# Products of a pair in program order, merges' stores on SyncE, convolution inputs five jobs apart: one change to a decoder trunk in Strassen-like pairs

## The chip, the cores and the metric

The kernel runs on one core of a Trainium2 chip. The metric is the time of one execution in device microseconds (us); lower is better. The program is compiled once, and the inputs are those of the reference.

## The reference, cut to what matters

One layer over a sequence of 1024 rows and a width of 1024, in f32: a layer norm with a shift and a scale from `c`, one wide input projection, three branches, a gated merge, an output projection and a last layer norm.

```python
u = layer_norm(x) * (1 + scale) + shift
proj = u @ w_in + b_in
a_v, a_g, b_b, b_c, b_h, b_g, c_a, c_b, c_g, merge = jnp.split(proj, SPLIT_IDX, axis=-1)
pooled = causal_multiscale_pool(a_v)                       # windows 2, 4, 8, 16
y_a = jnp.einsum("bsgi,gio->bsgo", pooled, pool_w).reshape(bsz, slen, W_BRANCH)
y_a = y_a * pool_scale * jax.nn.silu(a_g)
y_b = b_b * causal_dwconv(b_c * b_h, sc_w, sc_b) * jax.nn.silu(b_g)      # 3 taps
h_c = causal_dwconv(c_a * jax.nn.sigmoid(c_b), cf_w, cf_b)               # 31 taps
y_c = jax.nn.silu(layer_norm(h_c, cf_ln_g, cf_ln_b)) * jax.nn.silu(c_g)
m = sum(sigmoid(merge)[k] * (y_k @ w_branch[k]))                         # k = a, b, c
x_new = layer_norm(ALPHA * x + gate * (m @ w_out))
```

## The kernel before, in words

Channels lie on the 128 partitions, the sequence on the free axis. An f32 product is made of three TensorE matmuls: each operand is split into a high and a low part, and `mm3` (L129) multiplies low by high, high by low and high by high, 128x128 weights against 128x512 columns.

The work is a list of **jobs**. Four classic jobs come first (their order is written out by hand). Then come 46 **pairs**: each makes two blocks of 128 channels of the projection at once, with seven products where eight would be needed, from sums of weight blocks and sums of blocks of `u`. A product is 12 matmuls of 128x512 (four blocks of the contraction by three), so a pair is 84. The pairs are `b0`..`b7` and `d0`..`d7` (branch B), `c2`..`c7` (the inputs of the 31-tap convolution; the first two blocks are the classic jobs), `cg` (its gates), `a0`..`a7` (branch A) and `m` (merge gates). After the pairs come the merges: `z1_0`..`z1_7` with the four `pool` jobs between the first of them, then `z0_0`..`z0_7`, then `z2_0`..`z2_7` (the digit behind z is the branch: 0 is A, 1 is B, 2 is C; a z job is 48 matmuls, a pool job 24). Last come the output projection and the last norm.

A pair (class `Pair`, L434 to L542) has two parts. **Its weights** are made in `step` while an earlier pair multiplies: the raw columns come on the SyncE (SP) queue; VectorE (DVE) makes four sums of half tiles; for each of the weight tiles `wa`, `wb`, `wc` and `wd` ScalarE (ACT) writes the high part (L506) and VectorE the low part (L508). `wa`, `wb` and `wc` share one pool of three buffers. **Its products** (`run`, L520 to L542) go into three PSUM banks, `px`, `pz` and `py`. Between products the partial result is taken over: into the tiles `r1` and `r2` by ACT with the bias (L525, L530 and L534) or by DVE additions (L528, L536, L538). Six banks serve the pairs, so those of the pair after next take over those of this one; within a pair `px` is reused, first after A11 B11 (ACT, L525), then after S3 T3 (DVE, L536), and A22 T4 must wait for that addition.

The 31-tap convolutions are DVE work that has no place of its own: `conv_step` (L601) is called once after each job and issues `TAPS` = 6 taps (L610, each an operation on 128x1024) of the convolution at the head of a list; a convolution takes five jobs. Finished convolutions are summed: the first is copied on ACT into a new tile `hsum` (L620), the others are added by DVE, and each is stored to `h_dram`.

The order of instructions on each engine comes from the framework's scheduler, which sorts by dependencies and its own estimate of when each operand is there; `after(ins, mark)` adds a dependency and so an order. The jobs' order is a list built at L877 to L893: c pairs are put in at every `every`-th place.

The DMA queues concerned: all loads of weights are issued on SP. Loads of intermediate results and most stores are issued on POOL (`store`, L543, whose default is `nc.gpsimd`): pooled values and the gates `sga` back from DRAM (`a_load`, L654, with `load_split`, L732), `y` tiles for the merges (also L734), and the stores of `h_dram`, `pool_dram`, `g_dram`, `y_dram` and `c_dram`. A queue issues in order; a store that waits for its data holds what stands behind it. After the loads ACT makes the high part of each `y` or `pool` tile (L129), DVE the low part (L130). `c_rstd` (L800 and L210 to L214) makes the 1/std of branch C's norm, its last step on POOL.

Of the kernel before, what the change touches and what calls it, by code (L numbers as in the profile page):

```python
# [11 lines left out]
AF = mybir.ActivationFunctionType  # L12
# [7 lines left out]
NT = D // P  # L20
# [39 lines left out]
def kernel(  # L60
# [16 lines left out]
    nc = tc.nc  # L77
# [15 lines left out]
    LEFT, RIGHT = slice(0, HALF), slice(HALF, S)  # L93
    HALVES = (LEFT, RIGHT)

    def slot(name, dt=F32):
        return big.tile([P, D], dt, tag="big", name=name)
# [14 lines left out]
    marks = {}  # L112
# [19 lines left out]
    def mm3(ps, wh, wl, rh, rl, start, stop):  # L132
        for n, (w, r) in enumerate(((wl, rh), (wh, rl), (wh, rh))):
            nc.tensor.matmul(  # L134
                ps, w, r, start=start and n == 0, stop=stop and n == 2, skip_group_check=True
            )


    ident = const.tile([P, P], F32, name="ident")
# [308 lines left out]
    def bias(col):  # L448
        return bin_cols[:, col // P : col // P + 1]

    class Pair:
# [26 lines left out]
        def step(self, what):  # L478

            raw1, raw2 = self.raw  # L480
            a1, a2 = (r.rearrange("p (i q c) -> p q i c", q=2, c=P) for r in self.raw)
            if what[0] == "S":
                t = wsum.tile([P, 2, HALF], F32, tag="sum", name=f"s{what[1:]}_{self.name}")
                self.sums[what[1]] = t.rearrange("p n c -> p (n c)")
                one, two = (t[:, n].rearrange("p (i c) -> p i c", c=P) for n in range(2))
                if what == "S12":
                    nc.vector.tensor_add(one, a2[:, 0], a2[:, 1])
                    nc.vector.tensor_sub(two, one, a1[:, 0])
                    self.s2 = two
                else:  # L490
                    nc.vector.tensor_sub(one, a1[:, 0], a2[:, 0])
                    nc.vector.tensor_sub(two, a1[:, 1], self.s2)
                return
            which, high = what[1], what[2] == "h"
            if high and which == "d":
                self.w[which] = wlast.tile([P, 2, HALF], F32R, tag="last", name=f"wd_{self.name}")
            elif high:
                self.w[which] = wspl.tile([P, 2, D], F32R, tag="w", name=f"w{which}_{self.name}")
            hi, lo = (self.w[which][:, n] for n in range(2))
            if which == "d":  # L500
                src = a2[:, 1]
                hi, lo = (t.rearrange("p (i c) -> p i c", c=P) for t in (hi, lo))
            else:
                src = raw1 if which == "a" else self.sums["1" if which == "b" else "3"]
            if high:
                nc.scalar.activation(hi, src, AF.Identity)  # L506
            else:
                marks["split"] = nc.vector.tensor_tensor(  # L508
                    out=lo, in0=src, in1=f32(hi), op=ALU.subtract
                )  # L510

        def product(self, ps, left, right, first):
            which, block = self.left[left]
            w = self.w[which]
            for i in range(4):
                ks = slice(block(i) * P, (block(i) + 1) * P)
                rh, rl = quarter(right, i)
                mm3(ps, w[:, 0, ks], w[:, 1, ks], rh, rl, first and i == 0, i == 3)

        def run(self):  # L520
            col1, col2 = self.cols
            px, pz = bank(f"px_{self.name}"), bank(f"pz_{self.name}")
            r1, r2 = slot(f"r1_{self.name}"), slot(f"r2_{self.name}")
            self.product(px, "A11", "B11", True)
            nc.scalar.activation(r1[:, LEFT], px, AF.Identity, bias=bias(col1))  # L525
            py = bank(f"py_{self.name}")
            self.product(py, "A12", "B21", True)
            nc.vector.tensor_add(r1[:, LEFT], py, r1[:, LEFT])  # L528
            self.product(pz, "S1", "T1", True)
            marks["pair"] = nc.scalar.activation(  # L530
                r2[:, RIGHT], pz, AF.Identity, bias=bias(col2)
            )
            self.product(px, "S2", "T2", False)
            nc.scalar.activation(r1[:, RIGHT], px, AF.Identity, bias=bias(col1))  # L534
            self.product(px, "S3", "T3", False)
            nc.vector.tensor_add(r2[:, RIGHT], px, r2[:, RIGHT])  # L536
            self.product(pz, "S4", "B22", False)
            nc.vector.tensor_add(r1[:, RIGHT], pz, r1[:, RIGHT])  # L538
            self.product(px, "A22", "T4", False)
            self.after(r1, px, r2)  # L540

    def store(dst, src, q=None):  # L542
        return (q or nc.gpsimd).dma_start(out=dst, in_=src)  # L543
# [18 lines left out]
    conv = {"n": 0, "sum": None}  # L562
# [36 lines left out]
    def conv_step(n):  # L599
        while n > 0 and conv_todo:  # L600
            item = conv_todo[0]  # L601
            j, g, h, s = item
            w = cfw_cols[:, (K31 - 1 - s) * NT + j : (K31 - 1 - s) * NT + j + 1]
            if s == 0:
                h = item[2] = slot(f"h{j}")
                ins = nc.scalar.activation(h, g, AF.Identity, bias=vec("cf_b", j), scale=w)  # L606
                if j == 0:
                    after(ins, marks["u"])
            else:
                nc.vector.scalar_tensor_tensor(  # L610
                    out=h[:, s:], in0=g[:, : S - s], scalar=w, in1=h[:, s:],
                    op0=ALU.mult, op1=ALU.add,
                )
                n -= 1
            item[3] = s + 1
            if s == K31 - 1:
                conv_todo.popleft()
                if conv["sum"] is None:
                    conv["sum"] = slot("hsum")
                    nc.scalar.copy(conv["sum"], h)  # L620
                else:
                    nc.vector.tensor_add(conv["sum"], conv["sum"], h)
                store(h_dram[j], h)
                conv["n"] += 1
# [35 lines left out]
    def a_pool(g):  # L660
        def run(w):
            for o in range(2):
                ct = 2 * g + o
                ps = [bank(f"pool_ps{ct}_{h}") for h in range(2)]
                for i in range(2):
                    for h in range(2):
                        ph, pl = pooled[2 * g + i]
                        ws = slice((2 * i + o) * P, (2 * i + o + 1) * P)
                        mm3(
                            ps[h], w[:, 0, ws], w[:, 1, ws], ph[:, HALVES[h]], pl[:, HALVES[h]],  # L670
                            i == 0, i == 1,
                        )
                t = sg_a.pop(ct)
                for h in range(2):
                    nc.vector.scalar_tensor_tensor(  # L675
                        out=t[:, HALVES[h]], in0=ps[h], scalar=vec("pool_scale", ct),
                        in1=t[:, HALVES[h]], op0=ALU.mult, op1=ALU.mult,
                    )
                store(y_dram[0][ct], t)

        jobs.append(Job(f"pool{g}", pool_w[0][g], None, None, run=run))

# [81 lines left out]
    c_dram = dram_tiles("c_dram", NT)  # L764
# [5 lines left out]
    def c_square(j):  # L770
        t = c_state.pop(("h", j))
        nc.vector.tensor_sub(t, t, c_state["mean"])
        store(c_dram[j], t)
        sq = slot(f"sq{j}")
        nc.scalar.activation(sq, t, AF.Square)
        if j == 0:
            c_state["q"] = sq
        else:
            nc.vector.tensor_add(c_state["q"], c_state["q"], sq)
# [28 lines left out]
    def c_y(ct):  # L808
        n, sg = c_state.pop(("y", ct))
        nc.vector.tensor_mul(n, n, c_state["rb"])  # L810
        nc.scalar.activation(
            n, n, AF.Silu, bias=vec("cf_ln_b", ct), scale=vec("cf_ln_g", ct)
        )
        nc.vector.tensor_mul(n, n, sg)
        store(y_dram[2][ct], n)


    y, m, m_hi, m_lo, g_in = {}, {}, {}, {}, {}
# [38 lines left out]
    for b in (1, 0, 2):  # L857
        for i in range(NT // 2):
            light.append(
                lambda b=b, i=i: gates(  # L860
                    f"m{b}_{i}", C_M + b * D + 2 * i * P, AF.Sigmoid, g_dram[b][2 * i : 2 * i + 2],
                    nc.sync if (b, i) == (2, NT // 2 - 1) else None,
                )
            )
    heavy = [f for group in todo for f in group]
# [5 lines left out]
            order.append(light[li])  # L871
            li += 1
    order += light[li:]
    every = 6
    j = CLASSIC // 2
    for n, f in enumerate(order):
        if n % every == every - 1 and j < NT:  # L877
# [94 lines left out]
    for i, job in enumerate(jobs):  # L972
# [10 lines left out]
            f(*args)  # L983
        if 8 <= i < 8 + NT:
            gate_row(i - 8)
        if n_proj <= i < n_proj + 8 and (i - n_proj) % 2 == 0:
            a_load((i - n_proj) // 2)
        if i == n_a - 2:
            marks["y0"] = marks["split"]
            for k in range(NT):  # L990
# [91 lines left out]
```

## Time and profile before

| | us |
|---|---|
| median of three runs | 1385.55 (1384.88 to 1387.03) |
| the profiled execution | 1386.24 |
| its span (first to last instruction) | 1384.5 |
| PE busy in the span | 1330.3 (96%) |
| DVE busy | 1099.0 (79%) |
| ACT busy | 527.5 (38%) |
| POOL busy | 113.0 (8%) |

The span is cut in 40 slices in the profile, and PE's busy digits are 9 in nearly all of them; DVE's are 9 from about 35 to 450 us and 4 to 9 behind that. The share of DMA engines is under 5 tenths from about 70 to 970 us and 6 to 9 tenths for the 240 us behind it, where the merges load and store. A matmul's record shows its duration from start to modelled end, and matmuls overlap, so what a matmul costs is read from starts, or from a stretch divided by the number of them.

### The profile page before, as it was taken

The page shows a single profiled execution, that of the slowest core. Times are in us where ns is not written, and L with a number is a line of the kernel's source. Part 1 is how long each engine was busy: PE and PEld are TensorE (multiplying, and loading weights), DVE is VectorE, ACT ScalarE, POOL GpSimd, SP SyncE. Part 2 cuts the span into 40 slices and gives each one's busy share as a digit, 9 for nine tenths or more (in the row PEclk, how much of TensorE's full clock was granted, in tenths as well). Part 3 has the DMA queues.
Part 4 walks back from the last instruction along what each step waited for, and adds up shares of the span by engine and source line. Part 5 has one row for each costly group of instructions (what it writes and reads, how often), then busy time and mean ns, then how long its engine had stood idle before and what let it go on. Part 6 is the DMA issues. An engine that isn't in the chain of part 4 may idle for free. (4 is left out here: it accounts for less than half of the span.)

```text
span 1384.5 us, 15237 instructions
## 1 busy us (share of the span) xinstructions
PE 1330.3 (96%) x5893; PEld 1097.3 (79%) x5893; DVE 1099.0 (79%) x1292; ACT 527.5 (38%) x652; POOL 113.0 (8%) x220
## 2 busy tenths in 40 slices
PE   4999799999999999999999999999897999999997
PEld 3778688887888888888888888888685888888886
DVE  7999999999999589958975998699645657645576
ACT  6554244434443444435343543444422333313100
POOL 2000000000000000000000000000212232200010
PEclk9999999999999999999999999999998999999999
DMA  9511323443222313222342234224868979712332
GB/s 320 158 46 47 106 76 94 131 126 107 65 88 95 104 46 108 98 69 79 111 146 77 76 119 139 92 84 137 311 227 281 341 274 335 273 61 77 122 107 92
DMA packets 167949, 188.40 MB, mean 136 GB/s; under 512 B 6292, under 2 KB 138820, under 8 KB 167876
## 3 DMA queue, kind: packets, MB, share of 16 engines
q1 hardware_dynamic: 141936, 94.91, 23.1%
q0 software_dynamic: 25408, 92.29, 17.9%
q8 instruction: 46, 0.75, 0.2%
q10 hardware_dynamic: 532, 0.22, 0.1%
q14 instruction: 27, 0.22, 0.0%
HBM read 137.06 MB, written 50.34 MB: 135 GB/s over the span
## 5 line engine op out<-in xcount | busy, mean ns | idle before, releaser
L610 DVE SCALAR_TENSOR_TENSOR h<-r_c,cfw_cols,h 128x1023 f32<-128x1023 f32 (+9 forms) x180 | 226.9, 1261 | 5.5 <-ACT h L606 5.3
L610 DVE SCALAR_TENSOR_TENSOR h<-cs,cfw_cols,h 128x1023 f32<-128x1023 f32 (+29 forms) x60 | 75.8, 1263 | 1.3 <-ACT h L606 1.0
L832 DVE TENSOR_TENSOR g<-ps_z,g 128x512 f32<-128x512 f32 x48 | 31.7, 687 | 51.6 <-PE ps_z L134 51.1
L408 ACT ACTIVATE w_z<-raw_z 128x1024 fp32r<-128x1024 f32 x24 | 25.2, 1060 | 124.3 <-PE ps_z L134 62.3
L134 PE MATMUL ps_p<-u,w_p 128*128 128x512 f32 x192 | 48.8, 409 | 0.6 <-DVE u L346 0.6
L134 PEld LDWEIGHTS ps_p<-u,w_p 128*128 128x128 f32 x192 | 36.8, 196 | 8.8 <-DVE u L346 1.7
L414 DVE TENSOR_TENSOR w_z<-raw_z,w_z 128x1024 fp32r<-128x1024 f32 x24 | 29.1, 1220 | 14.6 <-ACT w_z L408 14.6
L543 POOL DMA_DIRECT2D g_dram<-r_m x22 | 11.7, 532 | 349.4 <-ACT r_m L718 238.1
L134 PE MATMUL py_m<-u,wa_m 128*128 128x512 f32 x144 | 36.2, 389 | 0.0
L134 PE MATMUL ps_z<-y_3h,w_z 128*128 128x512 f32 x96 | 34.0, 391 | 1.7 <-ACT y_3h L129 1.7
L134 PE MATMUL ps_z<-y_0h,w_z 128*128 128x512 f32 x96 | 35.4, 403 | 0.0
L134 PE MATMUL px_m<-u,wa_m 128*128 128x512 f32 x144 | 34.8, 389 | 0.0
L134 PE MATMUL pz_m<-u,wc_m 128*128 128x512 f32 x144 | 34.6, 389 | 0.0
L134 PE MATMUL ps_z<-y_1h,w_z 128*128 128x512 f32 x96 | 34.0, 389 | 0.0
L134 PE MATMUL ps_z<-y_2h,w_z 128*128 128x512 f32 x96 | 33.8, 389 | 0.0
L134 PE MATMUL ps_z<-y_4h,w_z 128*128 128x512 f32 x96 | 33.5, 389 | 0.0
L134 PE MATMUL ps_z<-y_7h,w_z 128*128 128x512 f32 x96 | 33.3, 389 | 0.0
L134 PE MATMUL ps_z<-y_6h,w_z 128*128 128x512 f32 x96 | 33.3, 389 | 0.0
L134 PE MATMUL ps_z<-y_5h,w_z 128*128 128x512 f32 x96 | 33.3, 389 | 0.0
L1032 DVE TENSOR_TENSOR og<-out_ps,gate_b 128x512 f32<-128x512 f32 (+1 forms) x18 | 11.1, 624 | 26.7 <-PE out_ps L134 13.4
L134 PE MATMUL px_m<-t_1h,wb_m 128*128 128x512 f32 x96 | 32.1, 389 | 0.0
L134 PE MATMUL pz_m<-t_0h,wb_m 128*128 128x512 f32 x96 | 31.5, 389 | 0.0
(567 smaller groups left out, 3879.7 us busy)
## 6 DMA issues: line engine op xcount, KB each, us to landing
raw_m<-in_w_in_dram SPq DMA_DIRECT2D x24, 512.0 KB, 4.0
raw_z<-in_w_branch_dram SPq DMA_DIRECT2D x24, 512.0 KB, 10.3
g<-g_dram POOLq DMA_DIRECT2D x24, 512.0 KB, 8.2
g_dram<-r_m POOLq DMA_DIRECT2D x22, 512.0 KB, 3.6
ada<-in_w_ada_dram SPq DMA_DIRECT2D x32, 256.0 KB, 6.4
raw_b<-in_w_in_dram SPq DMA_DIRECT2D x16, 512.0 KB, 4.0
raw_d<-in_w_in_dram SPq DMA_DIRECT2D x16, 512.0 KB, 4.0
raw_a<-in_w_in_dram SPq DMA_DIRECT2D x16, 512.0 KB, 4.0
```

Source lines behind the costliest of these rows:

```text
L134: nc.tensor.matmul(ps, w, r, start=start and n == 0, stop=stop and n == 2, skip_group_check=True)
L408: nc.scalar.activation(self.w[:, 0, : self.width], raw, AF.Identity)
L414: marks["split"] = nc.vector.tensor_tensor(out=lo, in0=raw, in1=f32(hi), op=ALU.subtract)
L543: return (q or nc.gpsimd).dma_start(out=dst, in_=src)
L610: nc.vector.scalar_tensor_tensor(out=h[:, s:], in0=g[:, : S - s], scalar=w, in1=h[:, s:], op0=ALU.mult, op1=ALU.add,)
L832: nc.vector.tensor_mul(g[:, HALVES[h]], ps[h], g[:, HALVES[h]])
L1032: nc.vector.tensor_mul(t, ps[q], final["gate"][:, sl])
```

## The change

It has six parts.

1. `chained` takes the place of `mm3` in a pair's products: the first matmul of each product depends on the last of the product before it, so that PE takes the products as the program lists them. In `run` the product S2 T2 and its eviction now stand ahead of S1 T1, which now stands between S2 T2 and S3 T3.
2. ACT's high parts of `wa`, `wb` and `wc` are kept in their program order (not `wd`).
3. The copy of the first finished convolution into `hsum` is gone; the convolution's own tile is the sum.
4. The stores of `y_dram[0]` (from the pool jobs), `c_dram` and `y_dram[2]` are issued on SP, and with them four of the `g_dram` stores of branch C's gates where it was two.
5. `every` is 5 where it was 6: pairs `c2` to `c7` come earlier, the last convolution is done six to seven jobs sooner, and what lies between them shifts.
6. `a_load(0..3)` is called one job earlier each.

```diff
+    def chained(ps, wh, wl, rh, rl, first, start, stop):
+
+        for n, (w, r) in enumerate(((wl, rh), (wh, rl), (wh, rh))):
+            ins = nc.tensor.matmul(
+                ps, w, r, start=start and n == 0, stop=stop and n == 2, skip_group_check=True
+            )
+            if n == 0 and first and "product" in marks:
+                after(ins, marks["product"])
+        if stop:
+            marks["product"] = ins
...
             if high:
-                nc.scalar.activation(hi, src, AF.Identity)
+                ins = nc.scalar.activation(hi, src, AF.Identity)
+                if "high" in marks and which != "d":
+                    after(ins, marks["high"])
+                if which != "d":
+                    marks["high"] = ins
...
-                mm3(ps, w[:, 0, ks], w[:, 1, ks], rh, rl, first and i == 0, i == 3)
+                chained(ps, w[:, 0, ks], w[:, 1, ks], rh, rl, i == 0, first and i == 0, i == 3)
...
+            self.product(px, "S2", "T2", False)
+            nc.scalar.activation(r1[:, RIGHT], px, AF.Identity, bias=bias(col1))
             self.product(pz, "S1", "T1", True)
             marks["pair"] = nc.scalar.activation(
                 r2[:, RIGHT], pz, AF.Identity, bias=bias(col2)
             )
-            self.product(px, "S2", "T2", False)
-            nc.scalar.activation(r1[:, RIGHT], px, AF.Identity, bias=bias(col1))
...
                 if conv["sum"] is None:
-                    conv["sum"] = slot("hsum")
-                    nc.scalar.copy(conv["sum"], h)
+                    conv["sum"] = h
...
-                store(y_dram[0][ct], t)
+                store(y_dram[0][ct], t, nc.sync)
...
-        store(c_dram[j], t)
+        store(c_dram[j], t, nc.sync)
...
-        store(y_dram[2][ct], n)
+        store(y_dram[2][ct], n, nc.sync)
...
-                    nc.sync if (b, i) == (2, NT // 2 - 1) else None,
+                    nc.sync if b == 2 and i >= NT // 2 - 2 else None,
...
-    every = 6
+    every = 5
...
-        if n_proj <= i < n_proj + 8 and (i - n_proj) % 2 == 0:
-            a_load((i - n_proj) // 2)
+        if n_proj - 1 <= i < n_proj + 7 and (i - n_proj) % 2 == 1:
+            a_load((i - n_proj + 1) // 2)
```

How the change moves instructions, at three places. A name's last number counts tiles; lines behind the change are 11 to 15 higher.

**ACT, at the first pair `b0`** (`r_b` are its results, `px_b` and `pz_b` its banks, `wd_b` its last weight tile; `wb_d` and `wa_c` are weights of the pair that follows). Before:

```order
L506 ACTIVATE wd_b_1248<-raw_b_1_1103 128x512
L557 ACTIVATE r_cg_1254<-px_cg_1251,bin_cols 128x512
L506 ACTIVATE wb_d_1370<-s_d_1367 128x1024
L620 COPY hsum<-h_955 128x1024
L525 ACTIVATE r_b_1384<-px_b_1382,bin_cols 128x512
L530 ACTIVATE r_b_1385<-pz_b_1383,bin_cols 128x512
L606 ACTIVATE h_1482<-cs_856,vec_cols,cfw_cols 128x1024
```

and now:

```order
L517 ACTIVATE wd_b_1248<-raw_b_1_1103 128x512
L572 ACTIVATE r_cg_1254<-px_cg_1251,bin_cols 128x512
L540 ACTIVATE r_b_1382<-px_b_1380,bin_cols 128x512
L517 ACTIVATE wa_c_1362<-raw_c_0_1229 128x1024
L545 ACTIVATE r_b_1382<-px_b_1380,bin_cols 128x512
L517 ACTIVATE wb_c_1368<-s_c_1365 128x1024
L547 ACTIVATE r_b_1383<-pz_b_1381,bin_cols 128x512
```

The copy into `hsum` stood between the weights of `d0` and the first eviction of `b0`; now only evictions and the weights of `c2`, which comes second, stand there.

**POOL's queue, at the loads for the third and fourth pool job** (`pool6l` is the pooled input of `pool3`, `sga` its gates, `y_dram` the stores of finished pool jobs). Before:

```order
L543 DMA y_dram_167<-sga_7152 128x1024
L543 DMA y_dram_168<-sga_7154 128x1024
L734 DMA pool5l<-pool_dram_194 128x1024
L658 DMA sga_7264<-sga_dram_201 128x1024
L658 DMA sga_7266<-sga_dram_202 128x1024
L827 DMA g_3_7316<-g_dram_224 128x1024
L543 DMA y_dram_169<-sga_7264 128x1024
L543 DMA y_dram_170<-sga_7266 128x1024
L768 DMA hc_7379<-h_dram_157 128x1024
L768 DMA hc_7381<-h_dram_158 128x1024
L734 DMA pool6l<-pool_dram_195 128x1024
```

and now:

```order
L748 DMA pool4l<-pool_dram_193 128x1024
L748 DMA pool5l<-pool_dram_194 128x1024
L672 DMA sga_7203<-sga_dram_201 128x1024
L672 DMA sga_7205<-sga_dram_202 128x1024
L841 DMA g_2_7212<-g_dram_223 128x1024
L748 DMA pool6l<-pool_dram_195 128x1024
L748 DMA pool7l<-pool_dram_196 128x1024
L672 DMA sga_7319<-sga_dram_203 128x1024
```

The stores of `y_dram` are gone from between the loads, and `pool6l` stands directly behind the gate load of the merge before it.

**DVE, at the pair `m0_3`, the eighth pair from the last** (`h` is a convolution under way, `r_m_3` the pair's result, `head` and `s_4` the pooling of an `a` pair). Now:

```order
L543 TENSOR_TENSOR r_m_3_5946<-py_m_3_5961,r_m_3_5946 128x512
L625 SCALAR_TENSOR_TENSOR h_5509<-r_c_5413,cfw_cols,h_5509 128x999
L656 TENSOR_TENSOR head_5911<-s_4_5908,inv_cnt 128x7
L625 SCALAR_TENSOR_TENSOR h_5509<-r_c_5413,cfw_cols,h_5509 128x998
L657 SCALAR_TENSOR_TENSOR s_4_5908<-s_4_5908,r_a_5806 128x1024
L625 SCALAR_TENSOR_TENSOR h_5509<-r_c_5413,cfw_cols,h_5509 128x997
L660 TENSOR_TENSOR s_4_5908<-head_5911,r_a_5806 128x7
L625 SCALAR_TENSOR_TENSOR h_5509<-r_c_5413,cfw_cols,h_5509 128x996
L625 SCALAR_TENSOR_TENSOR h_5509<-r_c_5413,cfw_cols,h_5509 128x995
L523 TENSOR_TENSOR wb_a_5932<-s_a_5929,wb_a_5932 128x1024
L625 SCALAR_TENSOR_TENSOR h_5509<-r_c_5413,cfw_cols,h_5509 128x994
L551 TENSOR_TENSOR r_m_3_5947<-px_m_3_5944,r_m_3_5947 128x512
```

Before, up to the same pair's addition from `px`:

```order
L642 TENSOR_TENSOR head_5759<-s_4_5756,inv_cnt 128x7
L508 TENSOR_TENSOR wd_m_3_5649<-raw_m_3_1_5495,wd_m_3_5649 128x512
L508 TENSOR_TENSOR wb_a_5780<-s_a_5777,wb_a_5780 128x1024
L610 SCALAR_TENSOR_TENSOR h_5357<-r_c_5261,cfw_cols,h_5357 128x1004
L643 SCALAR_TENSOR_TENSOR s_4_5756<-s_4_5756,r_a_5654 128x1024
L538 TENSOR_TENSOR r_m_3_5794<-pz_m_3_5793,r_m_3_5794 128x512
L487 TENSOR_TENSOR s_a_5907<-raw_a_1_5772 128x512
L610 SCALAR_TENSOR_TENSOR h_5357<-r_c_5261,cfw_cols,h_5357 128x1003
L646 TENSOR_TENSOR s_4_5756<-head_5759,r_a_5654 128x7
L488 TENSOR_TENSOR s_a_5907<-s_a_5907,raw_a_0_5770 128x512
L610 SCALAR_TENSOR_TENSOR h_5357<-r_c_5261,cfw_cols,h_5357 128x1002
L536 TENSOR_TENSOR r_m_3_5795<-px_m_3_5792,r_m_3_5795 128x512
```

Between the additions from `py` and from `px` stand six taps (the rows on `h`) and the end of a convolution is near; before there were four, one of them just ahead of the rows shown, with more of the weights' sums and low parts between them.

## Rows read from the trace of the kernel before

**Rows 1.** The page's first part: busy time, share of the span, instructions.
```profile
PE 1330.3 (96%) x5893; PEld 1097.3 (79%) x5893; DVE 1099.0 (79%) x1292; ACT 527.5 (38%) x652; POOL 113.0 (8%) x220
```

**Rows 2.** PE's waits: tile, releaser, us in total, times, longest.
```profile
PE pool_ps L134 <- ACT pool6h L129: 10.2, 1, 10.2
PE px_b L134 <- ACT r_b L525: 5.6, 1, 5.6
...
PE pz_d L134 <- DVE wb_d L508: 2.4, 1, 2.4
...
PE pool_ps L134 <- ACT pool0h L129: 1.7, 1, 1.7
```

**Rows 3.** Windows: length, PE, PEld, DVE, ACT, POOL busy (count), PEclk, DMA share, GB/s.
```profile
160.00:180.00 20.00, 11.97 (x37) 8.88 (x37) 17.05 (x17) 7.19 (x9) 0.53 (x1) 0.74 0.16 63
180.00:975.00 795.00, 795.00 (x3504) 656.93 (x3503) 691.32 (x763) 344.26 (x441) 32.90 (x62) 1.00 0.31 99
975.00:1000.00 25.00, 21.06 (x80) 15.31 (x79) 16.70 (x17) 11.98 (x13) 6.82 (x13) 0.93 1.02 386
...
1040.00:1070.00 30.00, 19.83 (x81) 16.01 (x80) 14.77 (x16) 7.75 (x9) 6.94 (x14) 0.83 0.81 279
```

**Rows 4.** Timeline of ACT around the first eviction of `b0`: start, duration, instruction, idle before.
```profile
171.86 1.04 ACT L620 COPY hsum<-h 128x1024 f32<-128x1024 f32 x1 [9.87 <-DVE h L610]
172.81 0.68 ACT L525 ACTIVATE r_b<-px_b,bin_cols 128x512 f32<-128x512 f32 x1
```

**Rows 5.** Timeline of DVE in the first pairs.
```profile
156.21 0.69 DVE L508 TENSOR_TENSOR wd_b<-raw_b,wd_b 128x512 fp32r<-128x512 f32 x1 [1.31 <-ACT wd_b L506]
...
193.21 0.68 DVE L488 TENSOR_TENSOR s_cg<-s_cg,raw_cg 128x512 f32<-128x512 f32 x1
193.81 1.22 DVE L508 TENSOR_TENSOR wc_c<-s_c,wc_c 128x1024 fp32r<-128x1024 f32 x1
194.94 1.27 DVE L610 SCALAR_TENSOR_TENSOR h<-cs,cfw_cols,h 128x1015 f32<-128x1015 f32 x1
196.13 0.68 DVE L491 TENSOR_TENSOR s_cg<-raw_cg,raw_cg 128x512 f32<-128x512 f32 x1
```

**Rows 6.** Timeline of POOL at the start of the merges and ahead of `pool3`.
```profile
975.10 0.54 POOL L543 DMA_DIRECT2D h_dram<-h  x1 [2.56 <-DVE h L610]
975.63 0.53 POOL L734 DMA_DIRECT2D y_3l<-y_dram  x1
...
1044.40 0.54 POOL L543 DMA_DIRECT2D y_dram<-sga  x1 [13.01 <-DVE sga L675]
...
1047.29 0.53 POOL L734 DMA_DIRECT2D pool6l<-pool_dram  x1
```

**Rows 7.** Timeline of ACT in the merges.
```profile
984.74 1.06 ACT L129 ACTIVATE y_3h<-y_3l 128x1024 fp32r<-128x1024 f32 x1 [2.61 <-DMA y_3l<-y_dram]
...
994.72 0.63 ACT L408 ACTIVATE w_pool<-raw_pool 128x512 fp32r<-128x512 f32 x1 [2.60 <-PE ps_z L134]
995.26 1.04 ACT L129 ACTIVATE pool0h<-pool0l 128x1024 fp32r<-128x1024 f32 x1
...
1057.19 1.06 ACT L129 ACTIVATE pool6h<-pool6l 128x1024 fp32r<-128x1024 f32 x1 [7.94 <-DMA pool6l<-pool_dram]
...
1122.09 1.06 ACT L129 ACTIVATE y_6h<-y_6l 128x1024 fp32r<-128x1024 f32 x1 [9.18 <-DMA y_6l<-y_dram]
```

**Rows 8.** Timeline of PE at the start of the first pool job.
```profile
996.35 1.94 PE L134 MATMUL pool_ps<-pool0h,w_pool 128*128 128x512 f32 x4 [1.72 <-ACT pool0h L129]
...
999.79 0.47 PE L134 MATMUL ps_z<-y_0l,w_z 128*128 128x512 f32 x1
```

**Rows 9.** Timelines of DVE and POOL at the 1/std of branch C.
```profile
1115.26 0.17 DVE L210 TENSOR_SCALAR c_rstd<-var_ps 128x8 f32<-128x8 f32 x1 [1.66 <-PE var_ps L785]
...
1115.51 2.61 POOL L214 TENSOR_TENSOR c_rstd<-c_rstd,neg_half 128x8 f32<-128x8 f32 x1 [18.08 <-DVE c_rstd L210]
1118.10 0.59 POOL L734 DMA_DIRECT2D y_6l<-y_dram  x1
```

## The prediction, made before the changed kernel ran

> **What bounds the kernel now.** I read the page's busy line first: PE has work in 96% of the span and no other engine more than 79% [rows 1]. So TensorE sets the time, and the only ways to change it are the stretches in which PE waits or runs at its lower clock. The windows show which these are. From 180 to 975 us PE is never idle: 3504 matmuls in 795.00 us, 0.2269 us each, at a granted clock of 1.00, which is the 2.4 GHz level [rows 3]. A product of 12 is then 2.72 us and a pair of 84 is 19.06 us. What any other window loses is its length less its matmuls at 0.2269. Next I read PE's waits, which name who was late [rows 2], and then the timelines of ACT, POOL and DVE around each, to see what stood ahead of the late instruction. Three windows lose time that the change can reach [rows 3]:
>
> - 160 to 180 us: 20.00 - 37 x 0.2269 = **11.6**. PE is idle 8.0 of it, and the clock was 0.74 on the mean, so the rest went at the half clock (1.2 GHz) after the idle time.
> - 975 to 1000 us: 25.00 - 80 x 0.2269 = **6.85**.
> - 1040 to 1070 us: 30.00 - 81 x 0.2269 = **11.6**, of which the wait on pool6h is 10.2 [rows 2].
>
> All times below are set against the profiled execution, 1386.24 us, which is 0.69 above the median of the runs.
>
> **What goes.** *The hsum copy.* The wait of 5.6 on r_b [rows 2] ends at ACT's eviction of px_b at 172.81. Directly ahead of it in ACT's queue stood the copy into hsum, which waited 9.87 us for DVE to finish the first convolution [rows 4]. The copy is gone, and no instruction that waits for a convolution takes its place. With the two products exchanged, px is also freed sooner. I take all 11.6 away, and put what DVE does in its place under A.
>
> *The start of the merges.* On POOL, y_3l's load stood behind a store of h that waited for DVE until 975.10 [rows 6], and y_3h started on ACT 2.61 us late [rows 7]. The convolutions now end several jobs sooner, and the last gate stores are on SP. That gives 6.85 less what stays. What stays is the wait on pool0h, 1.72, because on ACT the high part of the pool job's weights, which waits 2.60 for a matmul of the job before, still stands ahead of it [rows 7]. Behind that wait the 8 matmuls from 996.35 to 999.79 took 3.44 in place of 1.82, so 1.6 more at the half clock [rows 8]. So 3.3 stays and **3.5** goes.
>
> *The pool loads.* On POOL the load of pool6l, issued at 1047.29, stood behind two y_dram stores, the first of which had waited 13.01 us for DVE [rows 6]. Its ACT part began at 1057.19 after 7.94 us of waiting for that load [rows 7]. Now the stores are on SP and the load is called one job earlier. A z job and a pool job are 72 x 0.2269 = 16.3 us, more than the 10.2 that it was late. All **11.6** goes. SP's stores have weight loads behind them that are wanted two jobs on, so I cost that move at nothing. If that cover were gone, it would be a wait of the kind just removed.
>
> Sum removed: 11.6 + 3.5 + 11.6 = 26.7.
>
> **What comes.** First the prices of DVE, from one start to the next: a half tile 0.60 (193.21 to 193.81), a full tile 1.13, a tap 1.19 [rows 5]. An addition in the queue ahead of PE's need costs nothing, one behind too much work costs PE. The tightest place in a pair is A22 T4, which takes over px from S3 T3. Only the product S4 B22 lies between them, 2.72 us, of which the addition itself takes 0.69, so about 2.0 are free for whatever stands ahead of it.
>
> *A, the first pairs.* From the addition of b1 to that of d2, five pairs on, the changed order gives DVE 45 taps or like operations, 20 full and 40 half tiles: 45 x 1.19 + 20 x 1.13 + 40 x 0.60 = 100.2 us, where PE needs 5 x 19.06 = 95.3. DVE falls 4.9 behind, 2.9 beyond the free 2.0. It also waits for ACT now and then, as the 1.31 ahead of the wd_b low part shows [rows 5]; I take 1.0. With a half-clock stretch of 1.6 [rows 8], A is **5.5**. Nothing is the lower bound, if DVE enters the stretch with a lead. All of the 11.6 just removed is the upper bound, if DVE's work and not the copy was what held PE.
>
> *B, the end of the last convolution.* It now ends among a4, m0_3 and a5, with taps bunched. From a4's addition to m0_3's, DVE has 11 taps or like operations, 6 full, 8 half and three small ones of some 0.17 (as the c_rstd row [rows 9]): 13.1 + 6.8 + 4.8 + 0.5 = 25.2, against 19.06. It is 6.1 late, 4.1 beyond the free 2.0; with 1.6 for the clock, **5.7**. Bounds: 4.1, and 9.7, which is the 6.1 with the 3.6 of half-clock loss of the first window [rows 3] (11.6 - 8.0). Before, the same stretch held 6 taps, 4 full and 8 half, 16.5 us, and had slack.
>
> *C, the 1/std of branch C.* POOL's step of 2.61 stood ahead of y_6l and y_7l [rows 9]; in the new order it stands ahead of y_3l to y_7l. From DVE's c_rstd at 1115.26 to the start of y_6h took 6.8 [rows 7, 9]; with 1.06 for that part and some 1.3 for a split now ahead of c_rstd on DVE, a tile is ready after 9.2. PE has y_0 to y_2 to do meanwhile, 36 x 0.2269 = 8.2. So 1.0 late, **1.5** with a little half clock; bounds 0 and 8, the latter if the load also waits its turn as pool6l did.
>
> *D, the fixed order of products.* PE can no longer take a ready product ahead of one that is not, so each pair has a chain S1 T1, ACT's high part of wb (1.06), DVE's low part (1.22). The trace has such a wait once, 2.4 on wb_d [rows 2]. Elsewhere the weights are made a pair ahead. I take half of that, **1.2**. The lower bound is nothing; the upper is a small wait in each of the 46 pairs, the slower case below.
>
> The exchange of S1 T1 and S2 T2 itself adds no instruction, and ACT's kept order of high parts follows their use; both at nothing.
>
> **Sum:** 5.5 + 5.7 + 1.5 + 1.2 = 13.9. 1386.2 - 26.7 + 13.9 = 1373.4 as a profiled execution, less 0.7: **1373** as a median.
>
> **The rivals.** *DVE, not the copy, sets the first stretch.* The copy waited for DVE's taps, and DVE's digits are full there. If the stretch stays DVE-bound, A is 11.6: 1379. Against it: DVE is free for other work once evictions no longer wait.
>
> *The moved stores gain nothing.* In the merges' start the DMA engines are busy all of the time, and 0.81 of it from 1040 to 1070 [rows 3]. If pool6l is late for bandwidth and not for its place in the queue, 11.6 comes back: 1385, no change. The Trainium skill, page "DMA: Bandwidth & Descriptors", section "Issuing engines are not separate DMA queues", says that transfers started by different engines end up on the same 16 DMA engines and interleave, and that several issuers only save the time of issuing. By that rule the move to SP would yield nothing and this rival would be the forecast; but it does not speak of a store that waits for data at the head of an issuing queue, which is what held POOL to 1044.40 here [rows 6]. I take the row.
>
> *Slower: every pair waits at A22 T4.* PE's order is now fixed, and DVE's is too. If the addition of S3 T3 regularly finds a tap and a low part ahead of it, that is 1.27 + 1.22 = 2.49 by such rows [rows 5] against 2.03 free, 0.46 in each of 46 pairs, 21.2: with A, B and C, 1386.2 - 26.7 + 12.7 + 21.2 - 0.7 = 1393. It is slower from 0.37 us a pair upward. Against it: 795 us without one wait [rows 3] under an order that was nearly the same in most pairs.
>
> *Better.* If A, C and D hide altogether, B at 5.7 remains: 1364.5; with a small A, 1366.
>
> **How the numbers follow.** Chances: the forecast 0.50, better 0.17, DVE-bound first stretch 0.13, moved stores for nothing 0.08, slower 0.12. A measurement of this kernel can tell about 0.2%, 2.8 us: faster is below 1382.8, slower above 1388.3. The first three are faster, 0.80; the fourth is the same, 0.08; the last slower, 0.12. The range runs from 1364, the better case's end, to 1386, above the fourth case; the slower case and a few extremes are left out.
>
> **What the profile will show.** Right: no wait on r_b near 170 us, none on pool6h, none on y_3h; a wait of 1.7 on pool0h still there; small waits on DVE's r_d, r_b or cg additions between 180 and 300 us and at m0_3; a short wait on y_3h of branch A near the c_rstd. The forecast is wrong if PE is idle again at 160 to 200 us for over 5 us, if pool6h still waits, or if PE's waits list an addition some forty times with a few tenths each.

## The result and the profile after

The changed kernel takes 1370.22 us (median of 4 runs, 1367.52 to 1371.70), the kernel before beside it 1386.29 (4 runs). The ratio is 0.9883, 95% interval 0.9864 to 0.9901: faster by 16 us, where 1373 was forecast with a range of 1364 to 1386. The profiled execution took 1370.15, its span 1368.3.

PE's busy time on the page, which answers to [rows 1]:

```profile
PE 1327.2 (97%) x5893; PEld 1093.0 (80%) x5893; DVE 1099.5 (80%) x1292; ACT 531.7 (39%) x651; POOL 99.6 (7%) x194
```

PE's waits behind the head of the program, which answer to [rows 2]:

```profile
PE px_d L141 <- DVE r_d L551: 2.4, 2, 1.8
PE px_m L141 <- DVE r_m L551: 2.3, 1, 2.3
PE px_m L141 <- ACT r_m L540: 2.1, 1, 2.1
...
PE pool_ps L134 <- ACT pool0h L129: 1.7, 1, 1.7
...
PE px_c L141 <- DVE r_c L551: 1.6, 2, 1.0
...
PE ps_z L134 <- ACT y_3h L129: 0.4, 1, 0.4
```

The waits of 10.2 on pool6h, 5.6 on r_b and 2.4 on wb_d are gone. In their place stand waits of 2.3 and less on the partial results of pairs. The same windows as in [rows 3]:

```profile
160.00:180.00 20.00, 20.00 (x90) 16.55 (x89) 19.55 (x22) 9.59 (x12) 0.00 (x0) 1.00 0.12 29
180.00:975.00 795.00, 786.46 (x3454) 646.76 (x3453) 692.59 (x760) 343.77 (x436) 36.20 (x68) 1.00 0.33 104
975.00:1000.00 25.00, 23.22 (x100) 18.18 (x99) 16.19 (x16) 12.50 (x15) 6.34 (x12) 1.00 1.02 375
...
1040.00:1070.00 30.00, 30.00 (x133) 24.77 (x132) 17.10 (x18) 8.40 (x9) 4.22 (x8) 1.00 0.92 314
```

Three stretches that lost 30.1 us before hold 53, 20 and 52 matmuls more; what is still lost in them is the pool0h wait of 1.7 and the start behind it. The long window from 180 to 975 us, which had no idle time, holds 50 matmuls fewer. Idle times don't show all of a loss: behind a wait the first matmul takes 0.34 to the next start (206.54 to 206.88 at `d1`), where others take 0.23. So in the pairs I read the loss from starts. Under the fixed order a pair that waits for nothing takes 19.04 us from its A22 T4 to the next one's. Nine pairs lie between the first and the last of these rows of PE's timeline:

```profile
165.23 0.39 PE L141 MATMUL px_b<-t_1h,wd_b 128*128 128x512 f32 x1
...
323.32 1.88 PE L957 MATMUL gate_ps<-gacc,ones 128*1 128x512 f32 x4
...
344.34 0.39 PE L141 MATMUL px_cg<-t_1h,wd_cg 128*128 128x512 f32 x1
```

They took 179.11 in place of 171.36, and 0.2 was lost in the three pairs ahead: 8.0 by starts. But 1.8 of that (323.32 to 325.13) is no loss by the change. It is the row of gates for the last norm, four matmuls that the kernel before makes too, at 332.63. Without them term A is **6.2**, of which the idle times show 4.1. (The expectations of experiments 6 and 8 still count the 8.0.) At m0_3 and the pairs behind it, term B, the same reading gives **5.5**, of which 4.85 in m0_3.

**The ledger.** Gone, by the matmuls that the three windows hold more, at 0.2269 each: 12.0 + 4.5 + 11.8 = 28.3. Come: A 6.2, B 5.5, C 0.4, D nothing beside them, 12.1 in all. The head of the program, which the change does not touch, was 1.6 slower in this execution: at 100 us 351 matmuls were done in place of 358. That makes 14.6. PE's last matmul starts 14.45 earlier, before:

```profile
1374.15 0.28 PE L134 MATMUL out_ps<-wo7h,m7h 128*128 128x256 f32 x1
```

and now:

```profile
1359.70 0.28 PE L134 MATMUL out_ps<-wo7h,m7h 128*128 128x256 f32 x1
```

The end of the span comes 8.6 behind that matmul in place of 10.35, another 1.75. Together 16.2, where the two profiled executions differ by 16.1.

### The profile page after: what moved, and what is told of

The parts are those of the page before. It is cut to its first block, busy times and chain, and to the rows that moved or that the text cites. A ratio compares the mean times of both kernels' runs of the same rounds, so it can differ in the third digit from the quotient of the medians.

```text
span 1368.3 us, 15269 instructions
## 1 busy us (share of the span) xinstructions
PE 1327.2 (97%) x5893; PEld 1093.0 (80%) x5893; DVE 1099.5 (80%) x1292; ACT 531.7 (39%) x651; POOL 99.6 (7%) x194
## 5 line engine op out<-in xcount | busy, mean ns | idle before, releaser
L523 DVE TENSOR_TENSOR wb_m<-s_m,wb_m 128x1024 fp32r<-128x1024 f32 x12 | 14.7, 1224 | 28.9 <-ACT wb_m L517 28.9
L141 PE MATMUL px_m<-t_1h,wd_m 128*128 128x512 f32 x96 | 31.6, 391 | 2.3 <-DVE r_m L551 2.3
```

Of the source, the lines that this page charges most:

```text
L141: ins = nc.tensor.matmul(ps, w, r, start=start and n == 0, stop=stop and n == 2, skip_group_check=True)
L523: marks["split"] = nc.vector.tensor_tensor(out=lo, in0=src, in1=f32(hi), op=ALU.subtract)
```

## The experiments

Theory Q was the prediction's: queues whose head waited had held PE, and what comes back is DVE's load. The rivals were that DVE held the first stretch (D), that the fixed order makes the gain (P), and that the loads are late for bandwidth (W). Every ratio is to runs of the kernel before on the same chip; experiments 1 to 4 ran on one chip, where it took 1387.40, the others on a second one, where it took 1386.28 and 1386.88.

**1. The copy alone** (from the kernel before).

```diff
-                    conv["sum"] = slot("hsum")
-                    nc.scalar.copy(conv["sum"], h)
+                    conv["sum"] = h
```

> The kernel before, without the hsum copy alone (the first convolution's own tile is the sum). Theory Q (an instruction that waits at the head of ACT's or POOL's queue held PE, and what comes back is DVE's own load): the wait of 5.6 on r_b goes and small DVE waits of 3 to 8 us in all come in the first pairs, so 1376 to 1382. Rival D (DVE's work and not the copy held PE at 160 to 180 us): a wait of nearly the same length on another tile, 1384 to 1387. Rival P (the fixed order of products is what makes the time): no more than 3 us here.

1373.28, ratio 0.9892 (0.9877 to 0.9907): 14 us won by two lines. The window of the copy in this run:

```profile
160.00:180.00 20.00, 20.00 (x90) 16.58 (x89) 19.91 (x21) 7.67 (x10) 0.00 (x0) 1.00 0.18 55
```

Nothing is lost there, and no wait follows until 974 us, with DVE as busy as before. (The eviction that stood behind the copy is that of `b1`, the fourth pair, and the weights ahead of it are those of `d1`, where the sections above say `b0` and `d0`: A22 T4 of `b0` starts at 111.09, 62 us before that eviction.) Rivals D and P fall. So does a part of Q: the small DVE waits that I expected in the copy's place are not there. The pool6h wait, 8.4 here for 10.2, gives a further 1.8.

**2 and 3. The stores alone, and the earlier a_load alone** (each from the kernel before, with its lines of the diff shown above).

> The kernel before, with the stores of y_dram[0], c_dram, y_dram[2] and four of the g_dram stores on SP alone. pool6l still stands behind the two loads of hc, but no store of y_dram is ahead of it. Theory Q: the wait of 10.2 on pool6h falls below 3, 1375 to 1378. Rival W (the loads are late for bandwidth, whichever queue issues the stores): the wait stays at 8 to 12, 1384 to 1388.

> The kernel before, with a_load called one job earlier alone; the stores stay on POOL and pool6l now stands ahead of the stores of the third pool job. Theory Q: the wait on pool6h goes, and pool5l or pool7l behind a store may wait a little: 1374 to 1380. Rival W: a wait of 8 to 12 remains on one of the pool tiles, 1384 to 1388.

The stores: 1374.32, 0.9903 (0.9889 to 0.9918). The earlier call: 1378.24, 0.9929 (0.9915 to 0.9944). PE's waits in the merges, with the stores on SP:

```profile
PE pool_ps L134 <- ACT pool6h L129: 2.1, 1, 2.1
...
PE pool_ps L134 <- ACT pool0h L129: 1.7, 1, 1.7
...
PE ps_z L134 <- DVE y_4l L130: 0.4, 1, 0.4
PE ps_z L134 <- DVE y_5l L130: 0.4, 1, 0.4
```

and with the earlier call:

```profile
PE ps_z L134 <- ACT y_3h L129: 2.8, 2, 1.5
PE pool_ps L134 <- ACT pool0h L129: 1.7, 1, 1.7
```

Either of the two ends the wait on pool6h, wholly or but for 2.1, so they don't add up. Rival W falls: the same bytes move, and the DMA share from 1040 to 1070 even rises, from 0.81 [rows 3] to 0.92 after the whole change. The Trainium skill (page "DMA: Bandwidth & Descriptors", section "Issuing engines are not separate DMA queues") says that issuing from several engines saves only the time of issuing. By that rule the stores' move would have given next to nothing: two of them stood ahead of pool6l's load, and a store's issue on POOL takes 0.54 [rows 6]. The 13 us are measured. Most of it is the time in which POOL's queue stood at a store whose data was not there, 13.01 at one of them [rows 6]: the windows from 975 and from 1040 us hold 15 and 36 matmuls more than before, 11.6 us. Another 1.8 comes at the end of the span (see the last section).

**4. The changed kernel without its fixed order.**

```diff
-                chained(ps, w[:, 0, ks], w[:, 1, ks], rh, rl, i == 0, first and i == 0, i == 3)
+                mm3(ps, w[:, 0, ks], w[:, 1, ks], rh, rl, first and i == 0, i == 3)
```

> The changed kernel with its products ordered by the scheduler again (mm3, no chain); S1 T1 still stands behind S2 T2 in the program. Theory Q: the order by itself is worth little, 1366 to 1375, as PE had no wait from 180 to 975 us under the scheduler's order before. Rival P: most of the gain goes, 1379 to 1387.

1362.43, 0.9817 (0.9801 to 0.9833): 7.8 below the changed kernel (9 by the ratios), whose interval doesn't touch it, and below theory Q's range. I had the order at 1.2. Why it costs is seen at the pair that waited longest in the first stretch, d1. PE's timeline with the fixed order:

```profile
201.84 2.88 PE L141 MATMUL pz_d<-u,wc_d 128*128 128x512 f32 x12
206.54 0.50 PE L141 MATMUL px_d<-t_1h,wd_d 128*128 128x512 f32 x1 [1.82 <-DVE r_d L551]
```

and without it, after S2 T2 of the same pair:

```profile
195.91 0.39 PE L134 MATMUL px_d<-t_1h,wb_d 128*128 128x512 f32 x1
196.14 2.88 PE L134 MATMUL px_cg<-u,wa_cg 128*128 128x512 f32 x12
198.86 2.88 PE L134 MATMUL py_cg<-u,wa_cg 128*128 128x512 f32 x12
201.58 0.39 PE L134 MATMUL px_d<-t_0h,wc_d 128*128 128x512 f32 x1
...
204.30 2.88 PE L134 MATMUL pz_d<-u,wc_d 128*128 128x512 f32 x12
207.02 0.39 PE L134 MATMUL pz_cg<-t_0h,wb_cg 128*128 128x512 f32 x1
...
212.46 0.39 PE L134 MATMUL px_d<-t_1h,wd_d 128*128 128x512 f32 x1
```

With the scheduler's order the first two products of the next pair, cg1, stand between S2 T2 and S3 T3 of d1, and the next two between S4 B22 and A22 T4, the place of the wait. They need neither the banks nor the partial results of d1, so whoever takes over px has 5.4 us more each time. DVE is busy 691 to 696 us of the 795 in the kernel before, the changed one and this one; its load is about the same, and only in the fixed order PE meets much of its lag. Not all of the loss goes:

```profile
180.00:975.00 795.00, 792.52 (x3487) 652.96 (x3486) 695.54 (x765) 349.26 (x445) 41.28 (x78) 1.00 0.34 108
```

33 of the 50 matmuls are back, 7.5 us; 17 are not, with waits of 0.8 and less on several tiles.

**5. The fixed order without the exchange.** S1 T1 and its eviction back ahead of S2 T2.

> The changed kernel with S1 T1 back ahead of S2 T2, the fixed order of products kept. Theory F (by now: the fixed order by itself costs some 8 us, because PE can no longer fill a late operand's time with the next pair's products; the exchange only gives the eviction of px more time): with S1 T1 first, px has its eviction hidden behind a product but S3 T3 stands directly behind S2 T2 and waits for the eviction of px no more than before, as both write the same bank; S4 B22 on pz follows S3 T3. 1368 to 1378. Rival X (the exchange and not the order is what costs): 1360 to 1365, like the kernel without the fixed order.

1472.37, 1.0615 (1.0586 to 1.0644), 102 us above the changed kernel: a miss of both theories by far. ACT's timeline and then PE's in a pair at 500 us:

```profile
508.44 1.06 ACT L517 ACTIVATE wb_d<-s_d 128x1024 fp32r<-128x1024 f32 x1 [2.03 <-PE px_m L141]
509.40 0.67 ACT L549 ACTIVATE r_m<-px_m,bin_cols 128x512 f32<-128x512 f32 x1
```

```profile
510.12 0.50 PE L141 MATMUL px_m<-t_0h,wc_m 128*128 128x512 f32 x1 [1.72 <-ACT r_m L549]
```

S3 T3 takes over px directly behind S2 T2, and ACT first makes the next pair's high part, which waits for the end of S2 T2 too (its buffer), and only then evicts px. So 1.06 + 0.67 are open in every pair: PE waits at this place 46 times, 1.7 to 1.8 each, and most pairs take 21.1 in place of 19.04. Ten take 22.7 to 22.9; from 428 to 450 us, around one of them, the granted clock was 0.92, with no wait over 1.8:

```profile
428.00:450.00 22.00, 20.22 (x82) 16.23 (x81) 19.98 (x22) 7.93 (x10) 1.07 (x2) 0.92 0.30 96
```

With the exchange S1 T1 covers it. I had costed the exchange at nothing. Under a fixed order it is worth 102; under the scheduler's order nothing that can be told, as experiment 7 shows, which has S1 T1 first. ACT's kept order of high parts (part 2 of the change) is in this kernel too. Whether it helps to put the high part ahead of the eviction was not tested; no run takes it out alone from a kernel with the fixed order.

**6. Fewer taps a job, fixed order kept.** Two kernels: 5 taps in place of 6 up to job 16, and in the first of them also from job 37 on.

```diff
-            conv_step(TAPS if i < n_proj - 1 else NT * K31)
+            conv_step((5 if i < 17 or i > 36 else TAPS) if i < n_proj - 1 else NT * K31)
...
+            conv_step((5 if i < 17 else TAPS) if i < n_proj - 1 else NT * K31)
```

> The changed kernel with 5 convolution taps after a job in place of 6 for the first 13 calls that matter (jobs up to 16) and from job 37 on; the same taps in all, the last convolution ends three jobs later. Theory F with DVE's load as the cause of what the order exposes: one tap of 1.19 less per pair lifts the first pairs from 100 us of DVE work in five pairs to 94, below PE's 95.3, so the waits of 8.0 up to 345 us fall to under 3, and those of 5.5 at m0_3 to under 4: 1361 to 1366. Rival L (the fixed order waits on chains of latency, not on DVE's load): no gain, 1368 to 1372.

> The changed kernel with 5 taps after a job up to job 16 and 6 from there on. Theory: the first pairs lose 3.5 in place of 8.0, as with fewer taps at both ends; the end of the last convolution falls two jobs later, on pairs that carry a pooling of more steps, and loses between the 5.5 of the changed kernel and the 10.5 of the other tap kernel: 1365 to 1370, nearer the upper end if the pooling steps decide. Rival: with 6 taps at the end B stays at 5.5 and all of the 4.5 is won, 1364 to 1366.

1369.83, 0.9882 (0.9868 to 0.9897), and 1361.05, 0.9813 (0.9798 to 0.9829): the first in rival L's range, though not for its reason, the second below both ranges. By the pairs' lengths the first stretch loses 3.5 in both, for 8.0 before, or 1.7 for 6.2 without the row of gates: A is DVE's load, laid bare by the order. B goes up to 10.5 in the first and down to 2.8 in the second. PE's waits in the first:

```profile
PE px_m L141 <- ACT r_m L540: 4.4, 2, 2.4
PE px_a L141 <- ACT r_a L540: 2.0, 1, 2.0
PE px_a L141 <- DVE r_a L551: 0.9, 1, 0.9
```

and in the second:

```profile
PE px_m L141 <- ACT r_m L540: 1.9, 1, 1.9
```

A shift of the last convolution by one or two pairs changes B by several us. What DVE had to do in those pairs is told below, under B. Both expectations missed on B: in the first I had it fall to under 4, in the second stay above 5.5. The second kernel keeps the fixed order and is level with experiments 4 and 7, which don't have it: with less for DVE to do beside the first pairs, hardly anything of the order's price is left. What fewer taps give without the order was not run.

**7. Copy, stores and a_load only** (the kernel before with these three parts, so without the fixed order, the exchange, ACT's kept order and the new spacing).

> The kernel before with the copy gone, the stores on SP and a_load one job earlier, and nothing else. Theory F: as good as the changed kernel without its fixed order, 1360 to 1365, since the fixed order is the only other part with a price; the gains of the copy (14) and of the pool loads (9 to 13) add up, as they are 850 us apart. Rival E (convolution inputs five jobs apart are needed to clear the start of the merges): 1366 to 1371, with waits on y_3h and y_4h near 975 us.

1360.56, 0.9813 (0.9796 to 0.9829). Three parts give 26 us, more than the six together. It can't be told from experiment 4 (0.9801 to 0.9833), so the exchange, ACT's kept order and the spacing of five together bring nothing beside a free order. Two waits of 0.2 and 0.5 on y_4l and y_5l remain at the merges' start; rival E falls.

**8. Inputs six jobs apart, fixed order kept** (`every = 6`).

> The changed kernel with the convolution inputs six jobs apart again, fixed order kept. Theory: the loss in the first pairs stays (the same taps beside the same pairs, 6 to 9 us), and the last convolution ends at the last two pairs, where its store of h holds y_3l's load on POOL again, for 1 to 3 us; the bunching at m0_3 goes (its 5.5): 1366 to 1372. Rival: the spacing is what clears the merges' start, and without it 4 to 7 us come back there beside a wait at another pair: 1373 to 1380.

1378.42, 0.9935 (0.9920 to 0.9951): in the rival's range, for half of its reason. No wait on y_3h came back at the merges' start, but one at another pair did. A is 8.3 with the row of gates, as expected. m0_3, whose loss I had expected to go, loses 4.0, and the third pair from the last 8.6. ACT's timeline there:

```profile
929.63 0.19 ACT L652 COPY s<-s 128x4 f32<-128x4 f32 x1 [0.32 <-DVE s L653]
933.07 0.20 ACT L652 COPY s<-s 128x8 f32<-128x8 f32 x1 [3.25 <-DVE s L653]
933.18 0.68 ACT L540 ACTIVATE r_m<-px_m,bin_cols 128x512 f32<-128x512 f32 x1
```

PE waits 5.7 for that last eviction. It stands behind a copy of 8 columns that waits for DVE's pooling. This looks like the hsum copy in small, but DVE has no gap here: it is busy 28.39 of the 28.46 us up to this pair's addition, so without the copy PE would be expected to wait there. Experiment 9 tries it at m0_3.

**9. Those pooling copies on DVE** (from the changed kernel: `nc.vector.tensor_copy` in place of `nc.scalar.copy` at L652).

> The changed kernel with the small copies at the head of the pooling (L652, 1 to 8 columns) on DVE in place of ACT. Theory C (half of what is lost at m0_3 comes because ACT's eviction of px stands behind such a copy, which waits for DVE's pooling addition): the wait of 2.1 on r_m of L540 goes, the wait of 2.3 on the addition stays; 1367 to 1369. Rival: DVE is just late, and what ACT no longer waits for comes back at the addition; 1369.5 to 1371.5, with 4 to 5 us on r_m of L551.

1370.33, 0.9877 (0.9859 to 0.9894): no change, in the rival's range, and theory C falls for the changed kernel. At m0_3 PE still waits 1.8 for L540 (2.1 with the copies on ACT), and 2.8 at the addition (2.3): what goes at the first place comes at the second, as the rival had it, though not up to its 4 to 5. ACT's timeline:

```profile
828.50 1.06 ACT L517 ACTIVATE wa_a<-raw_a 128x1024 fp32r<-128x1024 f32 x1 [4.23 <-issue]
829.46 0.67 ACT L540 ACTIVATE r_m<-px_m,bin_cols 128x512 f32<-128x512 f32 x1
```

In the changed kernel the same row for wa_a reads `828.70` and names py_m as its releaser: this high part needs the buffer that A12 B21 is still reading, and stands ahead of the eviction of px, which could have run in the 2.7 that ACT stood idle there, beside that product. The copy was the second thing in line, not the first.

**10 and 11. The wait on pool0h.** On ACT, the high part of pool1's weights is put behind those of pool0's inputs; once on the kernel of experiment 4, once on that of 7.

```diff
+            if self.name == "pool1":
+                after(ins, marks["pool0"])
```

> The changed kernel with its products ordered by the scheduler and the high part of pool1's weights kept behind those of pool0's inputs on ACT. Theory: the wait of 1.72 on pool0h, there in every trace so far, goes: 1360 to 1361.5, against 1362.4 without the edit. Rival: pool0's inputs land late and ACT is held by them, so that the weights of pool1 or z1_2 are late instead: 1362 to 1368.

> The kernel before without the copy, with the stores on SP, a_load one job earlier and the high part of pool1's weights behind those of pool0's inputs: none of the fixed order, the exchange or the new spacing. Theory: 1360.6 less the 1.7 of the wait on pool0h, 1358 to 1359.5. Rival: the kept order takes from the y waits ahead of it what it gives, 1360 to 1361.

1359.79, 0.9807 (0.9790 to 0.9824), and **1356.85**, 0.9782 (0.9764 to 0.9799). The wait is gone in both, and the medians fall by 2.6 and 3.7, more than the 1.7 expected and below both theories' ranges. In the profiled executions a stretch of half clock went with the wait: in the window from 975 to 1000 us the granted clock is 0.93 in experiments 4 and 7 and 1.00 in these two. The intervals overlap with those of 4 and 7, so the sizes are rough. The second is the fastest of all, 30 us below the kernel before and 13 below the changed one; from 60 us to the end PE's waits in it are

```profile
PE px_b L134 <- DVE wc_b L510: 1.3, 1, 1.3
PE ps_z L134 <- DVE y_4l L130: 0.5, 1, 0.5
...
PE ps_z L134 <- DVE y_5l L130: 0.4, 1, 0.4
```

## Why the prediction was right

**The three gains held.** The hsum stretch gave its 11.6 (experiment 1). The pool loads gave 11.6, and experiments 2 and 3 show why: place in POOL's queue. The merges' start gave 4.5 for 3.5: pool0h's wait of 1.7 stayed, as forecast, but the half clock behind it did not. PE's timeline now, for [rows 8]:

```profile
993.95 1.19 PE L134 MATMUL pool_ps<-pool0h,w_pool 128*128 128x512 f32 x4 [1.72 <-ACT pool0h L129]
```

Four matmuls in 1.19 where they took 1.94. What brings the half clock is not settled. The same wait of 1.7 stands in experiment 1 behind three waits of 0.5 to 0.8 on y_3 and y_4, and in experiment 4 behind none for 62 us; the clock fell in the second. Their windows, in this order:

```profile
975.00:1000.00 25.00, 22.13 (x92) 16.61 (x92) 15.04 (x16) 9.11 (x10) 3.73 (x8) 1.00 0.73 279
```

```profile
975.00:1000.00 25.00, 23.21 (x94) 18.36 (x93) 16.09 (x17) 8.90 (x10) 2.67 (x6) 0.93 0.91 331
```

So that 4.5 came and not 3.5 is luck, as far as these runs show.

**The new losses sum to 12.1 for the 13.9 forecast.** A was 6.2 for 5.5, B 5.5 for 5.7, C 0.4 for 1.5, D nothing of its own kind for 1.2. The half clock of 1.6 that I put into A and into B did not occur: the granted clock stays 1.00 through waits of up to 2.3. The profiled execution took 3.3 less than the 1373.4 of the sum: the gains came out 1.6 higher, the losses 1.8 lower, the end was 1.75 shorter, which was not in the sum, and the head 1.6 slower, which makes 3.5.

**A and B are DVE's load, as predicted.** DVE's windows in the changed kernel, from b1's addition to d2's and from a4's to m0_3's:

```profile
163.46:264.31 100.85, 97.91 (x429) 79.86 (x427) 100.23 (x106) 41.82 (x50) 2.13 (x4) 1.00 0.32 97
...
818.53:843.48 24.95, 21.30 (x93) 17.00 (x91) 24.91 (x29) 8.44 (x12) 1.60 (x3) 1.00 0.31 106
```

DVE is busy almost without a gap, 100.23 for the 100.2 that I added up and 24.91 for 25.2. In the first five pairs PE lost 4.6 for the 5.5. The rest of A lies in pairs that the sum left out, 0.2 ahead of b1 and 1.3 behind d2.

**The step that failed in its reasons** is "D, the fixed order of products", put at 1.2 as a matter of weights made too late, with A and B costed apart from it. The order costs 7.8 (experiment 4), and it does so through A and B, whose sum falls with it. DVE's load decides how much (A falls from 6.2 to 1.7 with a tap less a pair), the order whether PE sees it. I took PE's freedom from 180 to 975 us under the scheduler's order as evidence against waits in a fixed one; experiment 4 shows that this order kept most of them away. So the rival "every pair waits" was argued away on the wrong ground. A wait in each of the 46 pairs does come in experiment 5, at another place (S3 T3 after S2 T2, on ACT) and at 2.1 a pair, and in the changed kernel the exchange, which I costed at nothing, keeps it off.

**B in the other kernels.** At m0_3 PE meets DVE's lateness at two places: 2.1 at the eviction of px, which stands on ACT behind a high part, and 2.3 at the addition. Experiment 9 shows that less at the first is more at the second. In the kernels with the fixed order the loss of a pair follows the time that DVE, without a gap, takes from the preceding pair's addition (of S3 T3) to this one's:

| kernel, pair | DVE, us | the pair lost, us |
|---|---|---|
| experiment 6, first kernel, m0_3 | 21.25 | 2.7 |
| experiment 6, second kernel, m0_3 | 22.35 | 2.2 |
| experiment 6, first kernel, a6 | 22.91 | 3.4 |
| experiment 8, m0_3 | 23.67 | 4.0 |
| changed kernel, m0_3 | 24.95 | 4.85 |
| experiment 9, m0_3 | 25.03 | 5.0 |
| experiment 8, third from the last | 28.46 | 8.6 |

This is read from the traces and was not tested by a run of its own. One loss does not fit: the pair behind a6 in the first kernel of experiment 6 loses 4.1 while DVE is idle for 5.3 of 21.60. There PE waits 2.4 for ACT's eviction, and the granted clock is 0.92.

**C** was 0.4 on y_3h, inside its bounds. The rivals that DVE sets the first stretch (D) and that the loads are late for bandwidth (W) were refuted by experiments 1 to 3.

## What to carry to other kernels

Look on each in-order engine for an instruction that waits for another engine and stands ahead of something that the bounding engine needs: a copy, a store or a cast of the next job's weights are the same case, and removing or moving one costs two lines. First see whether that other engine is late anyway: if it has no gap up to the next thing that is needed from it, the wait only moves there. Before fixing an order on the bounding engine, see whether its present order puts independent work between an operand's producer and its consumer; if so, that work is what hides the lag, and a fixed order needs an equal cover at every reuse of a bank. Test the parts of a change one by one even when the sum is faster: here three of six gave 26 us, and the other three took 10 of them back.

## What the runs showed that was not expected

Moving the stores to SP also shortened the end. From the start of the last matmul to the end of the span it takes 10.3 to 10.5 us in the three kernels that keep these stores on POOL (before, experiments 1 and 3), and 8.5 to 8.6 in the changed kernel and in experiments 2, 4 and 7. The last output stores are the same two on SP in all, and the last work on DVE has the same length: it ends 5.0 before the end of the span in the kernel before and 3.3 in the changed one. What happens in that time is not shown by the traces.

The lower clock level came behind long idle time: 0.74 on the mean in the window with 8.0 us of idle time, 0.83 in that with the wait of 10.2 [rows 2, 3]. It also came behind waits of 1.7 to 2.4 in experiments 4, 5 and 6 (0.92 and 0.93), and it did not in the changed kernel, with 1.00 in all four windows shown and waits of up to 2.3 in them. What decides between the two is not shown.
